# Output weights in half tiles from another queue, and loads and output products moved in program order, in the two feed-forwards of a two-layer block

## The chip, the cores and the metric

The kernel runs on one core of one Trainium2 chip. The metric is device time in microseconds, lower is better. Before the change three timed runs gave 1641.31, 1640.96 and 1637.72 us, median 1640.96.

## What is computed

A block of two layers works on 512 image positions `h` and 256 context positions `hc`, each of 1024 features, in float32. Each layer has a mixer (layer 0: a chunk MLP beside differential attention; layer 1: windowed attention with sinks) and a feed-forward. The change touches the feed-forwards alone:

```python
FFN_HIDDEN = ((8 * D_MODEL + 3 * 256 - 1) // (3 * 256)) * 256     # 2816
def swiglu(h, w_in, w_out):
    g, u = jnp.split(h @ w_in, 2, axis=-1)
    return (jax.nn.silu(g) * u) @ w_out
...
h = h + g2 * swiglu(modulate(h, norm2_g[l], sh2, sc2), ffn_w_in[l], ffn_w_out[l])
if need_ctx:                                                      # layer 0 only
    hc = hc + cg2 * swiglu(modulate(hc, norm2_g[l], csh2, csc2), ffn_w_in[l], ffn_w_out[l])
```

So layer 0's feed-forward has 768 columns (512 and 256), layer 1's 512.

## The kernel before

**Precision.** TensorE multiplies `float32r` tiles. Every float32 operand is split into a high part, which ScalarE makes by a copy that rounds, and a low part, the difference, which GpSimd or VectorE subtracts. One product of a 128-column block is then three matmuls (`mm3`, lines 100 to 102): high by high, high by low, low by high.

**Hidden features.** The 2816 hidden features are 22 groups of 128, numbered f. What the description of the change calls a pair is one f: the gate and the value columns of 128 hidden features, 1 MB of weights in one `raw` tile of 2048 columns, loaded on SyncE's queue by `ffn_in` (line 804). Layer 0 has two buffers for these tiles, layer 1 three (two in one pool, and one in the ring for each f with f % 3 == 2). Pairs 0 and 1 (layer 1: 0 to 2) go the direct way. All others use Strassen's scheme in Winograd's form: seven products, numbered 1 to 7, each of four column blocks, on half of the positions (384 columns in layer 0, 256 in layer 1). Their weights are `a11`, `a12`, `a21`, `a22` and four sums of them, which VectorE forms in `weights` (line 968). `slot` (lines 910 to 918) makes the high and low part of each: ScalarE's copy on line 913, the subtraction on line 917. There are 8 such slots in layer 0 and 12 in layer 1, so weights are made ahead of their products.

**Evacuations in a pair.** Products 1, 6, 7 and 4 accumulate in one half of a PSUM tile (`pw`), 5 and 3 in the other. Between them the running sum is read: after 1 on lines 996 and 997, after 5 on line 1005, after 6 on line 1001, after 3 on line 1008, after 7 on line 1012, after 4 on line 1017. The next product into the same half has to wait for that reading. After product 4 the hidden tile of the pair is split on lines 116 and 117 (`hh`).

**Output products.** `s2(g, m)` multiplies the two pairs 2g and 2g+1 with the block m (of 8) of the output weights, first the 512 positions, in layer 0 then the 256 of the context, and adds the result to the residual on line 766. Their weights come through `load` (lines 923 to 926): one `rawo` tile of 1024 columns (512 KB) for four m, in one buffer in layer 0 and two in layer 1, on SyncE's queue. `s2_weights` asks for it at m % 4 == 0 and makes a slot of 512 columns at every even m.

**Order.** For f from 3 to 21 a string gives the order in which products and output blocks are written down: `2156ab37cd4` for even f and `2a1b56c3d74` for odd f, where a digit is a product and a letter an output block (two at f = 3). The order on each engine is not this one, though: the program is built with `schedule_with_timeline_sim=True`, so a planner with a simulated clock of its own lays out each engine's queue, with the written order as its priority. What is ready in the plan can move ahead of what isn't. `tc.issue_after(ins)` binds this: an instruction in the block that runs on the same engine as `ins` is put behind `ins` in that engine's queue. At run time each queue is fixed.

**Beside it.** In layer 0's loop VectorE also computes the modulation of layer 1 (`ada_dot`, line 222) from 48 loads of 512 KB on SyncE's queue (line 216).

Of the kernel before, what the change touches and what calls it, by code (L numbers as in the profile page):

```python
# [6 lines left out]
F32 = mybir.dt.float32  # L7
F32R = mybir.dt.float32r
# [6 lines left out]
P = 128  # L15
# [6 lines left out]
NF = HID // P  # L22
# [4 lines left out]
class Builder:  # L27
# [821 lines left out]
    def ffn(self, l):  # L849
        tc, nc, a = self.tc, self.nc, self.a  # L850
        both = l == 0
# [4 lines left out]
        ring = tc.alloc_tile_pool(name=f"ring_f{l}", bufs=1, side="left", reuse_waits="tile")  # L856
        if both:

            for n, shape, bufs in (("rawo", [P, 1024], 1), ("hs", [P, T], 1), ("u", [P, NH], 1), ("w", [P, 1024], 5)):
                ring.tile(shape, F32, name=self.uid(n), tag=n, bufs=bufs)  # L860
        whos = ((0, TX), (TX, TC))[:2 if both else 1]
        todo = [(1, j, k) for j in range(6) for k in range(KT)] if both else []
# [47 lines left out]
        def slot(src, t=None):  # L910
            t = wtile() if t is None else t
            with tc.issue_after(self.first_sq.ins) if (3, 8)[l] <= self.nslot < 12 else ExitStack():
                nc.scalar.copy(t[:, 0, :], src)  # L913
# [3 lines left out]
            eng.tensor_tensor(t[:, 1, :], src, t[:, 0, :].bitcast(F32), ALU.subtract)  # L917
            return t
# [1 line left out]
        self.nslot = self.nw = 0  # L920
        self.first_sq = self.last_sq

        def load(src, cols):
            t = ring.tile([P, cols], F32, name=self.uid("rawo"), tag="rawo", bufs=(1, 2)[l])
            nc.sync.dma_start(t, src)
            return t

        def raw(f):
            return self.raws.pop(f) if f < 2 else self.ffn_in(l, f, ring if l and f % 3 == 2 else self.Rf)
# [26 lines left out]
            self.split(*hid[-1], gates.pop(f), nc.gpsimd)  # L956

        def weights(n, f):
            if f not in raws:
                raws[f] = raw(f)  # L960
                sums[f] = self.sumsq()[:, :512] if f % 3 == 2 else self.tmp("t")
            r, t = raws[f], sums[f]
            a11, a12, a21, a22 = [r[:, i * 512:(i + 1) * 512] for i in range(4)]
            for v, x, y, how in ((5, a21, a22, ALU.add), (6, t, a11, ALU.subtract), (3, a12, t, ALU.subtract),
                                 (7, a11, a21, ALU.subtract)):
                if v == n:
                    with tc.issue_after(self.last_diag.ins) if both and f < 3 and n == 5 else ExitStack():
                        nc.vector.tensor_tensor(t, x, y, how)  # L968
            return slot({1: a11, 2: a12, 4: a22}.get(n) if n in (1, 2, 4) else sums[f])
# [7 lines left out]
        def product(n, f):  # L977

            w = weights(n, f)
            st = state.setdefault(f, {})  # L980
            if n == 2:
                st["p2"] = (self.fill if f < 3 else self.bank)()[:, :NH]
                out = st["p2"]
            elif n == 1:
                w_ = self.wide()
                st["w"] = [w_[:, :NH], w_[:, 512:512 + NH]]
                out = st["w"][0]
            else:
                out = st["w"][n in (5, 3)]
            for j in range(4):  # L990
                c = slice(j * P, (j + 1) * P)
                self.mm3(out, (w[:, 0, c], w[:, 1, c]), op[n][j], j == 0 and n in (1, 2, 5), j == 3)
            ps0, ps1 = st.get("w", (None, None))
            if n == 1:
                g = st["g"] = self.gated_tile(ring if f % 3 == 2 else None)
                nc.scalar.copy(g[:, :NH], st["p2"])
                ins = nc.vector.tensor_tensor(g[:, :NH], g[:, :NH], ps0, ALU.add)
                more(1, f, ins)
                nc.scalar.activation(g[:, :NH], g[:, :NH], AF.Silu)
            elif n == 6:  # L1000
                nc.scalar.copy(st["g"][:, NH:], ps0)
            elif n == 5:
                own = f % 3 == 2
                st["u"] = ring.tile([P, NH], F32, name=self.uid("u"), tag="u", bufs=1) if own else self.tmp()[:, :NH]
                nc.scalar.copy(st["u"], ps1)
            elif n == 3:
                g = st["g"]
                ins = nc.vector.tensor_tensor(g[:, NH:], g[:, NH:], ps1, ALU.add)  # L1008
                more(3, f, ins)
                nc.scalar.activation(g[:, NH:], g[:, NH:], AF.Silu)  # L1010
            elif n == 7:
                ins = nc.vector.tensor_tensor(st["u"], st["u"], ps0, ALU.add)  # L1012
                more(7, f, ins)
                nc.vector.tensor_tensor(st["g"][:, NH:], st["g"][:, NH:], st["u"], ALU.mult)
            elif n == 4:
                g = st["g"]
                self.last_s1 = nc.vector.tensor_tensor(g[:, :NH], g[:, :NH], ps0, ALU.mult)
                hi, lo = self.hidden(F32R), self.hidden(F32R)
                if f < NF - 1:
                    self.split(hi, lo, g, nc.gpsimd)  # L1020
                else:
                    self.split(hi[:, NH:], lo[:, NH:], g[:, NH:])
                    self.split(hi[:, :NH], lo[:, :NH], g[:, :NH])
                hid.append((hi, lo))
                del state[f], raws[f], sums[f]
                more(4, f, self.last_s1)
# [5 lines left out]

        def s2_weights(g, m):

            if m % 4 == 0:
                outs[g] = load(a["ffn_out"][l, g, :, 256 * m:256 * m + 1024], 1024)
                if g == NF // 2 - 1:
                    f = NF + m // 4
                    pool = ring if l and f % 3 == 2 else self.Rf
                    self.big = pool.tile([P, 2048], F32R, name=self.uid("raw"), tag="raw", bufs=1 if pool is ring else 2)  # L1040
# [12 lines left out]

        hid, outs, w2, Wl = [], {}, {}, []

        nd = (2, 3)[l]
        self.direct_mm, self.gated = [], []
# [14 lines left out]
        for v in ("5 6 22 12 52 62 32 7 72 4 h 42", "5 6 d 4 7 h")[l].split():  # L1072
# [331 lines left out]
```

## Time and profile before

| | |
|---|---|
| timed runs, median | 1640.96 us (1637.72 to 1641.31) |
| profiled execution, span from first to last instruction | 1641.9 us (no time of its own is given beside the span) |
| mean granted clock of TensorE over the span | 0.977 |
| layer 0's loop | about 456 to 960 us of the span |
| layer 1's loop | about 1290 to 1600 us of the span |
| HBM read | 158.29 MB |

In the rows of the profile an instruction is named by its engine and its line in the kernel: PE is TensorE, PEld its weight loads, DVE VectorE, ACT ScalarE, POOL GpSimd, SP SyncE; `SPq` and `ACTq` are instructions that issue transfers. Names such as `w<-raw` say that a tile `w` is written from a tile `raw`. A bracket `[5.31 <-DMA raw<-ffn_in]` says how long the engine stood idle before the instruction and what ended that. In a view of waits, one row is "who <- whom: total us, times, longest us".

### The profile page before, as it was taken

What the parts mean: (1) busy time and instruction counts of PE and PEld (TensorE: products, weight loads), DVE (VectorE), ACT (ScalarE), POOL (GpSimd) and SP (SyncE); (2) the same over time, 40 slices, a digit from 0 to 9 for tenths busy, and PEclk for the clock granted to TensorE, in tenths of its full rate; (3) what the DMA queues carried; (4) which work ended last, traced back from release to release, by engine and by line L of the source; (5) the groups of instructions that cost most, each with busy time, mean ns of one, the idle gap of its engine ahead of it and who ended that gap; (6) DMA issues with size and microseconds to landing.
All of it is one profiled execution on the core that took longest, in us unless ns stands there. A gap on an engine that the chain in (4) does not pass through costs nothing.

```text
span 1641.9 us, 24642 instructions
## 1 busy us (share of the span) xinstructions
PE 1542.8 (94%) x9547; PEld 1367.1 (83%) x9547; DVE 1073.0 (65%) x1980; ACT 724.5 (44%) x1472; POOL 766.9 (47%) x543
## 2 busy tenths in 40 slices
PE   6999989999999999999999988999989999999996
PEld 4776877899899889998989978777868989898886
DVE  4621788756857788666665585665667857666665
ACT  2423675645533233333333244555664544444443
POOL 0463221062157666666666316532222466675662
PEclk9999989999999999999999999999999999999998
DMA  8744100141223343343432012110233222322201
GB/s 317 298 153 169 40 7 1 65 139 68 76 79 116 105 139 131 105 150 126 142 131 77 27 51 91 52 33 25 74 116 123 65 103 92 101 90 103 90 27 52
DMA packets 47957, 161.98 MB, mean 99 GB/s; under 512 B 5472, under 2 KB 9952, under 8 KB 40160
## 3 DMA queue, kind: packets, MB, share of 16 engines
q1 hardware_dynamic: 47696, 160.28, 28.4%
q8 instruction: 75, 1.23, 0.3%
q14 instruction: 42, 0.34, 0.1%
q10 hardware_dynamic: 144, 0.13, 0.0%
HBM read 158.29 MB, written 2.10 MB: 98 GB/s over the span
## 4 chain that ended last, share of the span: by engine, by line
PE 69%; DVE 11%; POOL 6%; DMA 5%; ACT 4%; issue 3%; POOLq 0%; SPq 0%; DVEq 0%; ACTq 0%
PE pw L100 9%; PE pw L101 9%; PE pw L102 9%; PE pb L100 7%; PE pb L101 7%; PE pb L102 7%; POOL w L917 5%; DMA raw<-ffn_in 3%; PE pf L100 3%; PE pf L101 2%; PE pf L102 2%; PE pb L1257 2%; PE pb L1246 2%; PE pf L351 2%; DVE t L968 2%
## 5 line engine op out<-in xcount | busy, mean ns | idle before, releaser
L100 PE MATMUL pw<-ax,w 128*128 128x384 f32 (+2 forms) x732 | 237.5, 328 | 16.1 <-DVE q L1012 6.7
L101 PE MATMUL pw<-ax,w 128*128 128x384 f32 (+2 forms) x732 | 237.9, 325 | 4.1 <-DVE ax L458 2.5
L78 POOL TENSOR_TENSOR w<-raw,w 128x512 fp32r<-128x512 f32 (+1 forms) x84 | 127.6, 1526 | 243.2 <-ACT w L75 220.8
L102 PE MATMUL pw<-ax,w 128*128 128x384 f32 (+2 forms) x732 | 236.7, 325 | 2.1 <-POOL w L917 2.1
L917 POOL TENSOR_TENSOR w<-raw,w 128x512 fp32r<-128x512 f32 x119 | 177.7, 1507 | 54.2 <-ACT w L913 53.4
L917 POOL TENSOR_TENSOR w<-t,w 128x512 fp32r<-128x512 f32 x90 | 133.4, 1482 | 139.9 <-ACT w L913 136.5
L100 PE MATMUL pb<-hh,w 128*128 128x512 f32 x480 | 167.3, 362 | 12.8 <-ACT hh L116 8.3
L766 DVE SCALAR_TENSOR_TENSOR xT<-pb,mod,xT 128x512 f32<-128x512 f32 (+3 forms) x208 | 144.5, 704 | 43.8 <-PE pb L102 43.1
L101 PE MATMUL pb<-hh,w 128*128 128x512 f32 x480 | 171.2, 358 | 0.5 <-POOL hh L117 0.5
L102 PE MATMUL pb<-hh,w 128*128 128x512 f32 x480 | 170.7, 357 | 0.0
L100 PEld LDWEIGHTS pw<-ax,w 128*128 128x128 f32 x732 | 142.0, 195 | 27.2 <-DVE q L1012 8.1
L100 PE MATMUL pw<-T,w 128*128 128x384 f32 (+1 forms) x508 | 159.1, 314 | 4.8 <-DVE hs L1008 2.4
L101 PE MATMUL pw<-T,w 128*128 128x384 f32 (+1 forms) x508 | 158.6, 312 | 4.0 <-DVE T L117 4.0
L102 PE MATMUL pw<-T,w 128*128 128x384 f32 (+1 forms) x508 | 158.2, 312 | 0.0
L101 PEld LDWEIGHTS pw<-ax,w 128*128 128x128 f32 x732 | 142.6, 195 | 12.1 <-DVE ax L458 3.4
L102 PEld LDWEIGHTS pw<-ax,w 128*128 128x128 f32 x732 | 142.4, 195 | 6.0 <-POOL w L917 2.7
L913 ACT CAST w<-t 128x512 fp32r<-128x512 f32 x104 | 64.5, 621 | 176.8 <-DVE t L968 122.5
L917 POOL TENSOR_TENSOR w<-rawo,w 128x512 fp32r<-128x512 f32 x63 | 94.1, 1493 | 66.5 <-ACT w L913 66.5
L100 PEld LDWEIGHTS pb<-hh,w 128*128 128x128 f32 x480 | 89.5, 189 | 27.0 <-ACT hh L116 10.8
L100 PEld LDWEIGHTS pw<-T,w 128*128 128x128 f32 x508 | 97.2, 192 | 9.7 <-DVE hs L1008 3.9
L101 PEld LDWEIGHTS pw<-T,w 128*128 128x128 f32 x508 | 97.4, 192 | 6.6 <-DVE T L117 4.6
L102 PEld LDWEIGHTS pb<-hh,w 128*128 128x128 f32 x480 | 90.3, 188 | 13.1
(363 smaller groups left out, 4056.7 us busy)
## 6 DMA issues: line engine op xcount, KB each, us to landing
raw<-ffn_in SPq DMA_DIRECT2D x44, 1024.0 KB, 4.9
ar<-ada SPq DMA_DIRECT2D x24, 1024.0 KB, 7.3
ar<-ada SPq DMA_DIRECT2D x48, 512.0 KB, 3.5
rawo<-ffn_out SPq DMA_DIRECT2D x44, 512.0 KB, 3.9
raw<-odd_out SPq DMA_DIRECT2D x32, 256.0 KB, 2.7
raw<-qk SPq DMA_DIRECT2D x16, 256.0 KB, 7.9
raw<-uv SPq DMA_DIRECT2D x16, 256.0 KB, 2.7
raw<-even_out SPq DMA_DIRECT2D x8, 512.0 KB, 4.2
```

Source lines behind the costliest of these rows:

```text
L78: eng.tensor_tensor(lo, raw, hi.bitcast(F32), ALU.subtract)
L100: mm(out, s[0], m[0], start=start, stop=False, **kw)
L101: mm(out, s[0], m[1], start=False, stop=False, **kw)
L102: return mm(out, s[1], m[0], start=False, stop=stop, **kw)
L351: nc.tensor.matmul(ps[32 * q:32 * q + 32, :w], cst[:, k, :], t[:, w * q:w * q + w], start=k == 0, stop=k == KT - 1, skip_group_check=True)
L766: self.nc.vector.scalar_tensor_tensor(h, ps[:, r], self.modcol(l, j, m, who), h, ALU.mult, ALU.add)
L913: nc.scalar.copy(t[:, 0, :], src)
L917: eng.tensor_tensor(t[:, 1, :], src, t[:, 0, :].bitcast(F32), ALU.subtract)
L968: nc.vector.tensor_tensor(t, x, y, how)
L1246: last = nc.tensor.transpose(pt[:, x * P:(x + 1) * P], es[2 * (x % 2) + x // 2][:, kb * P:(kb + 1) * P], self.ident)
L1257: nc.tensor.matmul(po[64 * h:64 * h + 64, :], V[vb][:, 64 * g:64 * g + 64], t[:, h * TC:h * TC + TC], start=kb == 0, stop=kb == nb - 1, sk ...
```

## The change

Three things, all in `ffn`. **Half tiles**: output weights are loaded in tiles of 512 columns (256 KB), two buffers in layer 0 and six in layer 1. One half is asked for ahead of the loop in layer 0, six in layer 1, and then one at each even m: in layer 0 before the slot of that m is made, from ScalarE's queue and behind the latest high-part copy of `slot` (`last_hi`); in layer 1 after it, from SyncE's queue. **Pairs ahead**: at the top of the loop body for f the weights of pair f+1 (layer 0) or f+2 (layer 1) are asked for; at f = 3 pairs 3 and 4, or 3 to 5. These loads are put behind the last weight load of the mixer (`last_w`) on SyncE's queue. **Program order**: every output product is put behind the last matmul of the product that is written ahead of it (`last_mm`) on TensorE. The outputs of the last two pairs (letters e to j, `s2_part` without `s2`) are not bound.

```diff
-            for n, shape, bufs in (("rawo", [P, 1024], 1), ("hs", [P, T], 1), ("u", [P, NH], 1), ("w", [P, 1024], 5)):
+            for n, shape, bufs in (("rawo", [P, 512], 2), ("hs", [P, T], 1), ("u", [P, NH], 1), ("w", [P, 1024], 5)):
...
-                nc.scalar.copy(t[:, 0, :], src)
+                self.last_hi = nc.scalar.copy(t[:, 0, :], src)
...
-        def load(src, cols):
-            t = ring.tile([P, cols], F32, name=self.uid("rawo"), tag="rawo", bufs=(1, 2)[l])
-            nc.sync.dma_start(t, src)
-            return t
+        def load():
+            g, c = halves.pop(0)
+            t = ring.tile([P, 512], F32, name=self.uid("rawo"), tag="rawo", bufs=nrawo)
+            with tc.issue_after(self.last_hi.ins) if both else ExitStack():
+                (nc.scalar if both else nc.sync).dma_start(t, a["ffn_out"][l, g, :, c:c + 512])
+            outs.append(t)
...
-            if f not in raws:
-                raws[f] = raw(f)
+            if f not in sums:
+                if f not in raws:
+                    raws[f] = raw(f)
                 sums[f] = self.sumsq()[:, :512] if f % 3 == 2 else self.tmp("t")
...
-                self.mm3(out, (w[:, 0, c], w[:, 1, c]), op[n][j], j == 0 and n in (1, 2, 5), j == 3)
+                self.last_mm = self.mm3(out, (w[:, 0, c], w[:, 1, c]), op[n][j], j == 0 and n in (1, 2, 5), j == 3)
...
-            if m % 4 == 0:
-                outs[g] = load(a["ffn_out"][l, g, :, 256 * m:256 * m + 1024], 1024)
-                if g == NF // 2 - 1:
+            if m % 4 == 0 and g == NF // 2 - 1:
...
-                w2[g] = slot(outs[g][:, m % 4 * 256:m % 4 * 256 + 512], t)
+                if both and halves:
+                    load()
+                w2[g] = slot(outs.pop(0), t)
+                if not both and halves:
+                    load()
...
-        def s2(g, m):
+        def s2(g, m, after):
 
             W = s2_weights(g, m)
-            for off, n in whos:
-                s2_part((2 * g, 2 * g + 1), m, W, off, n)
+            with tc.issue_after(after.ins):
+                for off, n in whos:
+                    s2_part((2 * g, 2 * g + 1), m, W, off, n)
...
+        nrawo = (2, 6)[l]
+        halves = [(g, c) for g in range(NF // 2) for c in range(0, 2048, 512)]
...
         for f in range(3, NF):
+            with tc.issue_after(self.last_w.ins):
+                for i in range(f if f == 3 else f + 1 + l, min(f + 2 + l, NF)):
+                    raws[i] = raw(i)
+                for _ in range(nrawo - both if f == 3 else 0):
+                    load()
...
-                        s2(*todo_m.pop(0))
+                        s2(*todo_m.pop(0), self.last_mm)
```

More of the change, by code (lines that the diff above doesn't have):

```diff
@@ L1033, in s2_weights @@
         def s2_weights(g, m):
-            if m % 4 == 0:
-                outs[g] = load(a["ffn_out"][l, g, :, 256 * m:256 * m + 1024], 1024)
-                if g == NF // 2 - 1:
-                    f = NF + m // 4
-                    pool = ring if l and f % 3 == 2 else self.Rf
-                    self.big = pool.tile([P, 2048], F32R, name=self.uid("raw"), tag="raw", bufs=1 if pool is ring else 2)
+            if m % 4 == 0 and g == NF // 2 - 1:
+                f = NF + m // 4
+                pool = ring if l and f % 3 == 2 else self.Rf
+                self.big = pool.tile([P, 2048], F32R, name=self.uid("raw"), tag="raw", bufs=1 if pool is ring else 2)
             if m % 2 == 0:
@@ L1043, in s2_weights @@
                 t = self.big[:, o:o + 1024].rearrange("p (a b) -> p a b", a=2) if g == NF // 2 - 1 else None
-                w2[g] = slot(outs[g][:, m % 4 * 256:m % 4 * 256 + 512], t)
+                if both and halves:
[3 more added lines that the diff above has]
+                    load()
             w = w2[g]
             return [(w[:, 0, c:c + P], w[:, 1, c:c + P]) for c in range(m % 2 * 256, m % 2 * 256 + 256, P)]
-        def s2(g, m):
+        def s2(g, m, after):
             W = s2_weights(g, m)
-            for off, n in whos:
-                s2_part((2 * g, 2 * g + 1), m, W, off, n)
-        hid, outs, w2, Wl = [], {}, {}, []
+            with tc.issue_after(after.ins):
+                for off, n in whos:
+                    s2_part((2 * g, 2 * g + 1), m, W, off, n)
+        hid, outs, w2, Wl = [], [], {}, []
+        nrawo = (2, 6)[l]
+        halves = [(g, c) for g in range(NF // 2) for c in range(0, 2048, 512)]
         nd = (2, 3)[l]
```

## The prediction

> **What bounds the kernel now.** I read the header of the page first, then the table by windows, and only then the waits.
>
> ```profile
> span 1641.9 us, 24642 instructions
> PE 1542.8 (94%) x9547; PEld 1367.1 (83%) x9547; DVE 1073.0 (65%) x1980; ACT 724.5 (44%) x1472; POOL 766.9 (47%) x543
> ```
>
> TensorE is busy 94% of the span, so what the change can bring is time in which TensorE stands still or runs slowly in the two feed-forwards. The table by windows sizes that. Its columns are the window, its length, and for PE, PEld, DVE, ACT and POOL the busy time with the count of instructions, then the granted clock, DMA share and GB/s. The first and third rows are stretches without a stall, the second and fourth are the parts of layer 0 and layer 1 that the edited loop fills, and the last lies behind one stall.
>
> ```profile
> 640.00:690.00 50.00, 50.00 (x288) 47.31 (x287) 34.70 (x52) 17.87 (x32) 32.61 (x22) 1.00 0.40 142
> 456.00:960.00 504.00, 487.76 (x2745) 456.94 (x2745) 345.30 (x516) 171.59 (x311) 304.38 (x197) 0.99 0.33 110
> 1361.00:1394.00 33.00, 33.00 (x230) 30.78 (x229) 22.75 (x34) 15.31 (x33) 22.30 (x17) 1.00 0.27 96
> 1290.00:1600.00 310.00, 296.37 (x1990) 272.80 (x1989) 201.00 (x287) 135.46 (x280) 203.40 (x145) 0.99 0.26 87
> 557.00:563.60 6.60, 5.86 (x18) 5.67 (x19) 1.44 (x4) 2.08 (x4) 3.13 (x2) 0.50 0.24 79
> ```
>
> Without a stall layer 0 takes 50.00/288 = 0.1736 us a matmul, so its 2745 would take 476.6 us of the 504: 27.4 us are lost, 16.2 of them idle (504 - 487.8). Layer 1 takes 33.00/230 = 0.1435 us, so 1990 take 285.5 of 310: 24.5 us are lost, 13.6 of them idle. The rest goes mostly in stretches like the last row, at a granted clock of 0.50. A microsecond of idle time thus stands for 27.4/16.2 = 1.7 us in layer 0 and 24.5/13.6 = 1.8 us in layer 1, and the **stock** that the change can draw on is 51.9 us.
>
> Who ended the idle time is in the waits of PE in these two windows (total, times, longest); three rows of layer 0, then four of layer 1:
>
> ```profile
> PE pb L100 <- ACT hh L116: 8.3, 6, 2.9
> PE pb L100 <- ACT hs L996: 4.1, 4, 1.6
> PE pw L100 <- ACT hs L1001: 1.8, 1, 1.8
> PE pw L100 <- DVE q L1012: 6.2, 3, 2.5
> PE pw L100 <- DVE u L1012: 4.7, 2, 2.4
> PE pw L100 <- DVE hs L1008: 1.8, 3, 0.8
> PE pw L100 <- ACT u L1005: 0.8, 1, 0.8
> ```
>
> No row names a weight or a DMA; they name short evacuations (L996 to L1017) and the split of the hidden tile (L116). The timeline shows why those are late, here for the wait at 1418 us:
>
> ```profile
> 1408.38 0.33 SPq L925 DMA_DIRECT2D rawo<-ffn_out  x1
> 1409.63 0.33 SPq L804 DMA_DIRECT2D raw<-ffn_in  x1
> 1416.99 0.69 DVE L968 TENSOR_TENSOR t<-raw 128x512 f32<-128x512 f32 x1 [5.31 <-DMA raw<-ffn_in]
> 1417.60 0.41 DVE L1012 TENSOR_TENSOR q<-q,pw 128x256 f32<-128x256 f32 x1
> 1418.07 0.39 PE L100 MATMUL pw<-ax,w 128*128 128x256 f32 x1 [2.53 <-DVE q L1012]
> ```
>
> DVE stood 5.31 us before L968, the sum of a later pair's weights, until its load landed. L1012, for which TensorE waited, is the next instruction on DVE and starts as soon as L968 is through. So the bound is **an urgent evacuation queued behind an operation that waits for a transfer**.
>
> **The change part by part.** *Layer 1, half loads.* The chain of waits gives the first and the last of four such loads in layer 1 (the one above is the second), and one of layer 0; the DMA issues (count, size, median to landing) give the usual times:
>
> ```profile
> 1342.64 7.43 DMA raw<-ffn_in
> ...
> 1542.53 7.04 DMA raw<-ffn_in
> ...
> 747.07 6.89 DMA raw<-ffn_in
> raw<-ffn_in SPq DMA_DIRECT2D x44, 1024.0 KB, 4.9
> rawo<-ffn_out SPq DMA_DIRECT2D x44, 512.0 KB, 3.9
> raw<-odd_out SPq DMA_DIRECT2D x32, 256.0 KB, 2.7
> ```
>
> The four took 7.0 to 7.4 us in place of 4.9, and a 512 KB `rawo` load had left 1.25 us ahead of the one above. Half the size ahead of it should leave half of the 2.4 us: 1.2 us. Four of the five waits on L1012 (10.9 us in all) become shorter by 4 x 1.2 = 4.8 us idle, 8.6 with the slow clock at 1.8. Bounds: nothing, if the same stalls turn up at other places, and all of it, 10.9 x 1.8 = 19.6. I take **-7**, between 4.8 and 8.6, since not every such wait need be followed by a slow stretch.
>
> *Layer 0, ScalarE.* Three waits follow a cast of `rawo` that stands in ACT's queue until its load lands:
>
> ```profile
> 606.59 0.62 ACT L913 CAST w<-rawo 128x512 fp32r<-128x512 f32 x1 [2.17 <-DMA rawo<-ffn_out]
> 609.34 0.85 PE L100 MATMUL pb<-hh,w 128*128 128x512 f32 x3 [1.28 <-ACT hh L116]
> 705.37 0.62 ACT L913 CAST w<-rawo 128x512 fp32r<-128x512 f32 x1 [1.96 <-DMA rawo<-ffn_out]
> 706.42 0.44 PE L100 MATMUL pw<-ax,w 128*128 128x384 f32 x1 [1.82 <-ACT hs L1001]
> 898.97 0.62 ACT L913 CAST w<-rawo 128x512 fp32r<-128x512 f32 x1 [1.14 <-DMA rawo<-ffn_out]
> 900.38 0.85 PE L100 MATMUL pb<-hh,w 128*128 128x512 f32 x3 [1.12 <-ACT hh L116]
> ```
>
> With one buffer of 1024 columns the next load cannot start before the last subtraction on the old one. With two halves the next is asked for one cast earlier: the loop's 19 pairs take 504 us and two halves each, so 13 us ahead, against 2.7 us for 256 KB. These waits should go: 1.28 + 1.82 + 1.12 = 4.2 us idle, 7.1 with the slow clock. Bounds 0 and 7.1; I take **-6**, since another wait may then be the last to end.
>
> *Layer 0, DVE.* The same picture as in layer 1 stands behind two waits on L116:
>
> ```profile
> 557.74 1.44 PE L100 MATMUL pb<-hh,w 128*128 128x512 f32 x3 [2.86 <-ACT hh L116]
> 753.99 0.69 DVE L968 TENSOR_TENSOR t<-raw 128x512 f32<-128x512 f32 x1 [2.77 <-DMA raw<-ffn_in]
> 756.06 0.85 PE L100 MATMUL pb<-hh,w 128*128 128x512 f32 x3 [2.35 <-ACT hh L116]
> ```
>
> The load took 6.89 us, 2.0 more than 4.9; half of it back, twice, is 2.0 idle, 3.4 at 1.7. Bounds 0 and 5.2 x 1.7 = 8.8. I take **-3**.
>
> *End of layer 1.* The chain waits there for the last output weights:
>
> ```profile
> 1576.93 3.67 DMA rawo<-ffn_out
> ```
>
> Six halves instead of two whole tiles let them start earlier. What TensorE lost there is the 0.8 on L1005 and the longest wait on L1008, 0.8: **-1.6** (bounds 0 and 1.6).
>
> *Weights asked for ahead.* In the waits of SyncE's queue in layer 0 (total, times, longest) the pair loads (L804) already wait for the buffer, not for being asked:
>
> ```profile
> SPq L804 <- POOL w L917: 24.4, 13, 3.3
> ```
>
> 13 pair loads of the loop's 19 leave at the moment when GpSimd frees the tile. The buffer count is unchanged, so asking one or two pairs ahead can start few of them sooner: **0**. What covers the loads is that weights are prepared well ahead (no row of PE's waits names one); without that each pair would wait up to 4.9 us.
>
> *ScalarE's issues.* Layer 0 issues 44 half loads from ACT. The one DMA that ACT issues now is this:
>
> ```profile
> 50.74 0.39 ACTq L303 DMA_DIRECT2D q<-lqk  x1
> L917 POOL TENSOR_TENSOR w<-t,w 128x512 fp32r<-128x512 f32 x52 | 80.9, 1556 | 81.1 <-ACT w L913 81.0
> ```
>
> 44 x 0.39 = 17 us more on an engine that is busy 171.6 us of 504. Queued behind each are the casts, evacuations and hidden splits of ACT. PE lost 14.2 us (8.3 + 4.1 + 1.8) to 171.6 us of ACT, 8%, so 17 us cost 1.4. The issue also waits until GpSimd has read the half two back; the second row (POOL idle 81 us for ACT's casts) says GpSimd runs close behind ACT, and the issue is put behind the latest cast, so that wait is mostly over. At worst each issue stands for one GpSimd operation, 44 x 1.56 = 69 us, 8% of it 5.5. I take **+2**, range 0 to 7.
>
> *Output products in program order.* The fence on PE adds no semaphore wait; it forbids that output matmuls run ahead of the pair's own products. Gain: at most the 8.3 us on L116, already mostly counted. Loss: products 1, 6, 7 and 4 share one accumulator, and between them TensorE needs other work while ACT and DVE read it. The nearest row for an uncovered read is L1008, 1.8/3 = 0.6 us; for all 38 pairs of the two loops that would be 22.8 us. Output matmuls now also stand between 6 and 3 and between 7 and 4, where they cover. I take one pair in six: **+4**, range -8 to +23.
>
> Sum: -7 - 6 - 3 - 1.6 + 0 + 2 + 4 = **-11.6 us** on the profiled span of 1641.9, 1630.3. The median of the timed runs is 0.9 below that span, so 1640.96 - 11.6 = **1629** us.
>
> One rule speaks against a part of this sum. The Trainium skill, "DMA: Bandwidth & Descriptors", section "Issuing engines are not separate DMA queues", says that transfers started from ScalarE and SyncE run on the same DMA engines and interleave, so that a second issuer saves only issue time. The rows above are all of one issuer and cannot show it for layer 0. By it the -3 of layer 0 would be nothing, and the sum -8.6.
>
> **The rivals.**
>
> *No change.* Halves are two loads of 2.7 in place of one of 3.9, so the pair load may meet just as much traffic, and L968 stands before L1012 because the plan of the build put it there, which the edit does not forbid. Then -7 and -3 fall away: -6 - 1.6 + 2 + 4 = -1.6, **1639**. This is also the case in which asking ahead does nothing. For it: the waits of layer 1 recur in one pattern, every 66 us, so they come from the plan. Against it: the landing must be late for a wait, and the one shown was late behind a whole `rawo`. The same page, section "Measured (HBM→SBUF, 128 partitions, SWDGE, issued from GpSimd)", advises transfers of 1 MiB and more, which speaks for this rival; no run here shows it for halves yet.
>
> *Most stalls go.* L968 no longer lands in front of an evacuation: -19.6 - 7.1 - 8.8 - 1.6 + 2 = -35, **1606**. For it: the stall-free rows above, at a clock of 1.00. Against it: DVE and ACT keep every operation that waits.
>
> *Slower: the outputs no longer fill in.* Before, output matmuls may run wherever a product's accumulator is being read; fenced, TensorE has nothing else when the next product isn't ready. It decides when the cover of 12 product matmuls (12 x 0.1435, 1.7 us in layer 1) is shorter than the way through ACT and DVE, where L1012 alone takes 0.41, and their queues. Price: 38 x 0.6 = 22.8, with +2 for ScalarE, less 6, 3 and 1.6, and layer 1's -7 not had: +14.2, **1655**. For it: layer 1's L1012 waits already follow a row of products without outputs. Against it: in the stall-free stretches PE is busy 33.00 of 33.00 us with the same products.
>
> **How the numbers follow.** Forecast 43%, most stalls go 13%, no change 22%, slower 22%. The forecast's own range is 1620 to 1636. About 0.2% (3.3 us) is what a measurement of this kernel can tell from no change: faster is 0.43 + 0.13 + 0.06 of the middle case, which spreads over the line at 1637.7, **0.62**; within, **0.13**; slower, 0.22 + 0.03, **0.25**. Half of each end case lies outside 1608 to 1655, 0.07 + 0.11, so that is the range.
>
> **What would show it.** Right: PE's waits on L1012 in layer 1 fall from 10.9 to about 6 us; no wait on L1001 or L116 behind a `rawo` cast; layer 0's window loses about 7 us, layer 1's about 5 to 9; pair loads still leave when GpSimd frees them, usually in 4.9 us. Wrong: pair loads still land in 7 us in front of an evacuation; ACT stands at its own DMA issues waiting for POOL; PE idles in many small pieces on L997, L1001, L1008 or L1012; or DVE's waits on `raw` turn up at other instructions with the same total.

## The result, and the profile after

After the change the kernel takes **1653.85 us** (median of 4 runs, 1652.18 to 1656.48), before it 1639.47 (4 runs, 1637.72 to 1641.31): ratio 1.0083, 95% interval 1.0064 to 1.0102. It is 14.4 us slower where the prediction said 12 us faster. The time lies inside the range, 1 us from the rival "the outputs no longer fill in" (1655).

The header of the page after, then its table by windows for the same two stretches (columns as in the prediction):

```profile
span 1654.7 us, 24721 instructions
PE 1543.4 (93%) x9547; PEld 1359.4 (82%) x9547; DVE 1080.7 (65%) x1980; ACT 724.2 (44%) x1472; POOL 775.4 (47%) x543
```

```profile
456.00:960.00 504.00, 479.05 (x2656) 444.65 (x2656) 338.49 (x495) 163.81 (x298) 314.54 (x196) 0.99 0.33 108
1290.00:1600.00 310.00, 291.40 (x1960) 264.62 (x1959) 206.01 (x288) 138.56 (x283) 199.48 (x142) 1.00 0.26 86
```

TensorE does the same work (1543.4 us busy against 1542.8), but in the same 504 us of layer 0 it gets through 2656 matmuls instead of 2745, in layer 1's 310 us through 1960 instead of 1990. At the prediction's 0.1736 and 0.1435 us a matmul these would be 15.5 and 4.3 us, but the windows are fixed in time, and the later kernel has other work in them. The last matmul of product 7 is cleaner: it ends at 937.8 us before and 947.4 after in layer 0, at 1612.2 and 1625.1 in layer 1, so most of the loss lies in layer 0.

Where it stands is in the groups by line. Four groups hold the first matmuls (line 100) of the edited loops, and some from other parts of the program: `pw<-T` are products 5, 6 and 7, `pw<-ax` 1, 3 and 4, `pb<-ax` product 2, `pb<-hh` the outputs. A row gives busy time, mean ns, then the idle time ahead of the group and what ended it. Before:

```profile
L100 PE MATMUL pw<-ax,w 128*128 128x384 f32 (+2 forms) x732 | 237.5, 328 | 16.1 <-DVE q L1012 6.7 <-DVE u L1012 4.7 <-ACT hs L1001 1.8
L100 PE MATMUL pb<-hh,w 128*128 128x512 f32 x480 | 167.3, 362 | 12.8 <-ACT hh L116 8.3 <-ACT hs L996 4.1 <-DVE xT L766 0.2
L100 PE MATMUL pw<-T,w 128*128 128x384 f32 (+1 forms) x508 | 159.1, 314 | 4.8 <-DVE hs L1008 2.4 <-ACT T L116 1.6 <-ACT u L1005 0.8
L100 PE MATMUL pb<-ax,w 128*128 128x256 f32 (+1 forms) x320 | 98.0, 307 | 0.9 <-DVE ctxT L766 0.8
```

After (the lines have moved by three: L999 and L1000 evacuate after 1, L1008 after 5, L1004 after 6, L1011 after 3, L1015 after 7, L1020 after 4):

```profile
L100 PE MATMUL pw<-ax,w 128*128 128x384 f32 (+2 forms) x732 | 234.1, 324 | 8.5 <-DVE q L1015 3.7 <-ACT ax L194 1.6 <-ACT hs L1004 1.5
L100 PE MATMUL pb<-hh,w 128*128 128x512 f32 x480 | 167.1, 358 | 1.3 <-DVE xT L766 1.2
L100 PE MATMUL pw<-T,w 128*128 128x384 f32 (+1 forms) x508 | 164.0, 323 | 36.0 <-ACT q L1008 13.1 <-DVE hs L1011 9.7 <-DVE hs L1000 8.8
L100 PE MATMUL pb<-ax,w 128*128 128x256 f32 (+1 forms) x320 | 98.3, 308 | 5.4 <-ACT w L913 2.9 <-DVE ctxT L766 2.4
```

The waits that the prediction wanted shorter are shorter: those on L116 (8.3) are gone, those on L1012 (6.7 + 4.7, now L1015) are 3.7 + 1.2. Which part of the change did that is settled below. The loss is in one group, **products 5, 6 and 7: 4.8 us idle became 36.0**. In layer 0's window PE's waits (total, times, longest) are led by

```profile
PE pw L100 <- ACT q L1008: 9.3, 8, 2.7
PE pw L100 <- DVE hs L1000: 7.3, 7, 2.4
...
PE pw L100 <- ACT u L1008: 2.3, 3, 1.1
```

The timeline shows one of them; start and length in us, and in brackets the idle time before:

```profile
661.20 0.34 PE L102 MATMUL pw<-T,w 128*128 128x384 f32 x1
661.37 0.83 ACT L116 CAST hh<-hs 128x768 fp32r<-128x768 f32 x1 [1.20 <-DVE hs L1020]
662.11 0.47 ACT L1008 COPY q<-pw 128x384 f32<-128x384 f32 x1
662.63 0.44 PE L100 MATMUL pw<-T,w 128*128 128x384 f32 x1 [1.10 <-ACT q L1008]
```

The first row is the last matmul of product 5, the last row the first of product 6. Nothing stands between them on TensorE, so it waits 1.10 us while ScalarE finishes L116 and then copies what 5 left. The copy reads the half that 5 wrote, and 6 writes **the other half**. The description of the kernel ahead of the prediction had said that only the next product into the same half waits; in the program as it is built the wait goes by the whole tile, so six of a pair's seven products (1, 5, 6, 3, 7, 4) form one chain with an evacuation between every two.

In layer 1 the longest total is on L1011, the sum after 3 (8.6 us in eight waits). Each time that sum is the next instruction on VectorE behind a weight sum (L971) that stood 0.7 to 2.4 us for GpSimd's subtraction (L917). It is the prediction's picture of an urgent evacuation in a queue behind something that waits, here for GpSimd in place of a transfer.

**Theory.** Each product on the tile waits for the evacuation of the one before it. Free outputs, and products of the neighbouring pair, stood between them before; the fence with the letters `2156ab37cd4` and `2a1b56c3d74` leaves nothing between 5 and 6. Counted from the order of the built programs, with 2.0 us wanted between two products in layer 0 and 1.4 in layer 1 (a choice, a little under one product's 12 matmuls, 2.1 and 1.7), the matmul time that is missing, summed over 39 pairs, is (layer 0 and layer 1):

```text
              between 5 and 6    all five steps
before          1.4    0.0         15.9    3.6
after          30.7   13.8         41.8   20.8
```

**Rivals.** The change's other parts (ScalarE's issues, half loads, early requests) cost the time; or an order by hand costs by itself, whatever stands between the products.

### The profile page after: what moved, and what is told of

It reads as the page before. It is cut to its first block, busy times and chain, and to the rows that moved or that the text cites. A ratio compares the mean times of both kernels' runs of the same rounds, so it can differ in the third digit from the quotient of the medians.

```text
span 1654.7 us, 24721 instructions
## 1 busy us (share of the span) xinstructions
PE 1543.4 (93%) x9547; PEld 1359.4 (82%) x9547; DVE 1080.7 (65%) x1980; ACT 724.2 (44%) x1472; POOL 775.4 (47%) x543
## 4 chain that ended last, share of the span: by engine, by line
PE 63%; DVE 16%; POOL 6%; ACT 6%; issue 5%; DMA 4%; ACTq 0%; POOLq 0%; SPq 0%; DVEq 0%
PE pw L100 8%; PE pw L101 7%; PE pw L102 7%; PE pb L100 7%; PE pb L101 7%; PE pb L102 7%; POOL w L917 4%; DMA raw<-ffn_in 3%; PE pf L100 2%; PE pf L101 2%; PE pf L102 2%; PE pb L1270 2%; PE pb L1259 2%; DVE t L971 2%; DVE junk L222 2%
## 5 line engine op out<-in xcount | busy, mean ns | idle before, releaser
L100 PE MATMUL pw<-ax,w 128*128 128x384 f32 (+2 forms) x732 | 234.1, 324 | 8.5 <-DVE q L1015 3.7
L101 PE MATMUL pw<-ax,w 128*128 128x384 f32 (+2 forms) x732 | 234.6, 321 | 2.7 <-DVE ax L458 1.4
L102 PE MATMUL pw<-ax,w 128*128 128x384 f32 (+2 forms) x732 | 233.1, 320 | 0.0
L917 POOL TENSOR_TENSOR w<-t,w 128x512 fp32r<-128x512 f32 x90 | 129.3, 1437 | 159.6 <-ACT w L913 142.5
L917 POOL TENSOR_TENSOR w<-raw,w 128x512 fp32r<-128x512 f32 x119 | 177.6, 1505 | 49.7 <-ACT w L913 46.7
L100 PE MATMUL pw<-T,w 128*128 128x384 f32 (+1 forms) x508 | 164.0, 323 | 36.0 <-ACT q L1008 13.1
L766 DVE SCALAR_TENSOR_TENSOR xT<-pb,mod,xT 128x512 f32<-128x512 f32 (+3 forms) x208 | 144.0, 703 | 44.5 <-PE pb L102 44.2
L101 PE MATMUL pw<-T,w 128*128 128x384 f32 (+1 forms) x508 | 159.1, 313 | 2.9 <-DVE T L117 2.9
L102 PE MATMUL pw<-T,w 128*128 128x384 f32 (+1 forms) x508 | 158.9, 313 | 0.0
L100 PEld LDWEIGHTS pw<-ax,w 128*128 128x128 f32 x732 | 138.7, 190 | 21.7 <-DVE q L1015 5.4
L101 PEld LDWEIGHTS pw<-ax,w 128*128 128x128 f32 x732 | 139.3, 190 | 11.0 <-DVE ax L458 3.1
L102 PEld LDWEIGHTS pw<-ax,w 128*128 128x128 f32 x732 | 139.3, 191 | 3.0
L100 PEld LDWEIGHTS pw<-T,w 128*128 128x128 f32 x508 | 97.7, 192 | 50.0 <-ACT q L1008 17.2
L117 POOL TENSOR_TENSOR hh<-hs,hh 128x768 fp32r<-128x768 f32 (+1 forms) x42 | 80.5, 1917 | 70.6 <-ACT hh L116 69.2
L100 PE MATMUL pb<-ax,w 128*128 128x256 f32 (+1 forms) x320 | 98.3, 308 | 5.4 <-ACT w L913 2.9
L917 POOL TENSOR_TENSOR w<-rawo,w 128x512 fp32r<-128x512 f32 x63 | 94.1, 1494 | 18.4 <-ACT w L913 18.4
L102 PEld LDWEIGHTS pb<-hh,w 128*128 128x128 f32 x480 | 90.3, 188 | 13.9
```

The source lines that it names most:

```text
L100: mm(out, s[0], m[0], start=start, stop=False, **kw)
L101: mm(out, s[0], m[1], start=False, stop=False, **kw)
L102: return mm(out, s[1], m[0], start=False, stop=stop, **kw)
L117: return (lo_eng or nc.vector).tensor_tensor(lo, src, hi.bitcast(F32), ALU.subtract)
L766: self.nc.vector.scalar_tensor_tensor(h, ps[:, r], self.modcol(l, j, m, who), h, ALU.mult, ALU.add)
```

## The experiments

All ran with the kernel before on the same chip. e1 to e4, e5 to e8 and e9 to e12 each shared one chip, so a difference in us between these sets, or with the kernel after, goes across chips. "idle" is the sum of the four groups above, from one profiled execution each; e10's took 1607.66 us and e8's 1624.15, off their medians.

| kernel | us, median | ratio to before (95%) | idle, us |
|---|---|---|---|
| before | 1639.5 to 1642.3 | 1 | 34.6 |
| after | 1653.85 | 1.0083 (1.0064 to 1.0102) | 51.2 |
| e1 after, no fence | 1635.33 | 0.9965 (0.9953 to 0.9977) | 36.1 |
| e2 before, with fence | 1658.67 | 1.0106 (1.0087 to 1.0125) | 46.4 |
| e3 after, one output a gap | 1671.16 | 1.0181 (1.0166 to 1.0196) | 60.3 |
| e4 before, pairs ahead | 1639.13 | 0.9988 (0.9975 to 1.0000) | 36.2 |
| e5 after, two tiles | 1612.75 | 0.9821 (0.9796 to 0.9846) | 18.5 |
| e6 after, fence one earlier | 1641.41 | 1.0001 (0.9982 to 1.0020) | 41.9 |
| e7 after, every step covered | 1628.02 | 0.9911 (0.9890 to 0.9932) | 31.5 |
| e8 e1, SyncE's queue | 1630.23 | 0.9923 (0.9899 to 0.9946) | 26.6 |
| e9 before, two tiles | 1615.19 | 0.9852 (0.9830 to 0.9875) | 21.8 |
| e10 e5, no fence | 1599.71 | 0.9761 (0.9738 to 0.9784) | 14.1 |
| e11 e10, SyncE's queue | 1603.51 | 0.9776 (0.9757 to 0.9796) | 14.2 |
| e12 e5, SyncE's queue | 1614.60 | 0.9838 (0.9816 to 0.9859) | 23.6 |

### The parts of the change: e1, e2, e4

e1 is the kernel after, with the outputs free again:

```diff
-            with tc.issue_after(after.ins):
+            with ExitStack():
                 for off, n in whos:
```

> The whole change but for the fence: output matmuls may again run ahead of the pair's own products. Theory (the fence takes the cover from the products of one pair, which wait for each other's evacuation): the loss goes, 1632 to 1641 us, and PE's waits on the copies and sums of products 1, 5 and 3 are back to a few us in the two loops (31 us in the changed kernel on these three, 4.1 + 2.4 + 0.8 on them before). Rival A (the half loads from ScalarE's queue, or the reshuffled loads, cost the time): still 1650 to 1658. Rival B (asking ahead): still 1650 to 1658.

e2 is the kernel before with that fence alone (`last_mm` and `issue_after` in `s2`, nothing else).

> The kernel before with the fence alone: whole output tiles on SyncE's queue, pairs asked for as before. Theory: 1652 to 1665 us, as slow as the changed kernel or slower, with the same waits on the evacuations of 5, 3 and 1. Rivals A and B: within 3 us of the kernel before, 1637 to 1643.

e4 is the kernel before with the early requests alone (the loop at the top of the body for f, without the half loads).

> The kernel before with the pairs' weights asked for 1 or 2 pairs ahead, nothing else. The order on SyncE's queue changes by two loads at the start of layer 1. Theory: no change, 1636 to 1643 us, since pair loads leave when their buffer is freed. Rival B: 1648 us or more.

The fence costs 18.5 us beside the rest of the change (1653.85 - 1635.33, across chips) and 17.8 without it (1658.67 - 1640.86, the kernel before on that chip). The rest of the change gains 5.5 us (1640.86 - 1635.33), asking ahead nothing that can be told. The group of products 5, 6 and 7 follows the fence; e1, then e2 (where L1005 is the copy after 5):

```profile
L100 PE MATMUL pb<-hh,w 128*128 128x512 f32 x480 | 167.4, 361 | 19.4 <-ACT hh L116 13.0 <-ACT hs L999 4.0 <-DVE xT L766 2.1
L100 PE MATMUL pw<-T,w 128*128 128x384 f32 (+1 forms) x508 | 159.1, 313 | 6.3 <-DVE hs L1011 4.0 <-DVE hs L1000 1.8 <-ACT T L116 0.5
```

```profile
L100 PE MATMUL pb<-hh,w 128*128 128x512 f32 x480 | 166.9, 357 | 1.3 <-DVE xT L766 1.2
L100 PE MATMUL pw<-T,w 128*128 128x384 f32 (+1 forms) x508 | 163.1, 321 | 34.6 <-ACT q L1005 12.1 <-DVE hs L997 8.5 <-DVE hs L1008 8.1
```

They also show who removed the waits on L116: not the half loads (13.0 us in e1, more than before) but the fence, which keeps an output from running up against a hidden tile that isn't split yet. It saves them and pays more elsewhere. The waits on the sum after 7, 11.4 us before, are 4.2 with the fence alone (e2) and 6.8 with the rest alone (e1), so either shortens them.

### Same fence, other places for the outputs: e3, e6, e7

e3 puts one output after each product from 5 on:

```diff
-            for v in ("2156ab37cd4", "2a1b56c3d74", ...
+            for v in ("215a6b3c7d4", "215a6b3c7d4", ...
```

> The whole change with the fence kept, and the written order of pairs 3 to 20 changed to 215a6b3c7d4 for even and odd f, so that an output block stands between each product and the next that uses the same accumulator tile from 5 on. By the program's order the matmul time that is missing between two products of one tile falls from 41.8 to 9.4 us in layer 0 and from 20.8 to 3.7 us in layer 1 (counted against 2.0 and 1.4 us a step). Theory: the waits on 5 to 6 and 7 to 4 go, 1625 to 1638 us. Rivals A and B, or a fence that costs through anything but cover: 1648 to 1658.

A miss: it is the slowest kernel of all. The count behind that expectation had left out that the evacuation after 1 (a copy of product 2, then the sum with 1) needs product 2 as well, and here 2, 1 and 5 follow one another in every pair. The wait went there:

```profile
L100 PE MATMUL pw<-T,w 128*128 128x384 f32 (+1 forms) x508 | 165.8, 327 | 55.2 <-DVE hs L1000 46.3 <-ACT u L1008 3.8 <-DVE hs L1011 3.6
```

The wait for 5's evacuation (13.1 + 4.3 us in the kernel after) is down to 3.8 + 1.0, as it should be with an output between 5 and 6. In layer 1 some 12 us of the waits on L1000 also stand behind a weight sum (L971) that waited for its load. So the time speaks against the theory unless that hole in the count explains it; e7 closes the hole: there the next pair's products 2 and 1 (N and M) are written at the end of this pair.

```diff
-            for v in ("2156ab37cd4", "2a1b56c3d74", "2a1b56c3de7f4ghij", "2a1b56c3de7f4g")[...]:
+            for v in ("21" if f == 3 else "") + ("5a6b3c7NdM4", "5a6b3c7N4Md", "5a6b3cde7f4ghij", "5a6b3cde7f4g")[...]:
...
+                elif v in "NM":
+                    product(2 if v == "N" else 1, f + 1)
```

> The kernel after with its fence, but the order by hand rewritten: products 2 and 1 of the next pair are asked for at the end of this pair, and one output stands between every two products on the tile. Missing matmul time by the same count, now with product 2 counted as well: 5 us and 2 us. Theory (only cover counts): 1620 to 1638, likeliest 1630; PE's waits on L1000, L1008, L1011 and L1015 under 10 us in all. Open is the hidden tile, which the first output of every second pair needs one product earlier than before: waits on L116 of up to 2 us in ten pairs a layer would bring it to 1645. Rival (order by hand costs by itself): 1648 or more, with the four rows at over 25 us.

Within the expectation, 26 us less than after with the same fence. The waits on the four lines sum to 16.7 us, more than the 10 hoped for, and product 2 now waits 7.8 us for outputs that VectorE has not read yet (L766):

```profile
L100 PE MATMUL pb<-hh,w 128*128 128x512 f32 x480 | 169.3, 359 | 1.9 <-DVE xT L766 1.4 <-ACT hh L116 0.2
L100 PE MATMUL pw<-T,w 128*128 128x384 f32 (+1 forms) x508 | 158.7, 313 | 15.4 <-DVE hs L1000 5.0 <-DVE hs L1011 5.0 <-ACT u L1008 4.6
```

e6 loosens the fence of the kernel after by one product:

```diff
-                        s2(*todo_m.pop(0), self.last_mm)
+                        s2(*todo_m.pop(0), self.prev_mm)   # last matmul of the product before the last one
```

> The kernel after, with the fence one product looser: output matmuls may not run ahead of the last product but one, where they may not run ahead of the last product in the kernel after. So the planner can again put outputs between two products on one tile. Counted from the program's order as before (matmul time missing between one product and the next on its tile, 2.0 us wanted in layer 0, 1.4 in layer 1): 22 us and 3 us, against 42 and 21 in the kernel after and 18 and 4 without the fence. Theory: 1633 to 1643, likeliest 1637. Rival (any fence on outputs costs, since they are no longer free to fill a random gap): between the two, 1643 to 1652.

Within the expectation: 12 us of the fence's 18 come back. Against before it stands at 1.0001, e1 at 0.9965, and the intervals don't touch: a rest of some 6 us remains. In its rows the waits on 5's evacuation (L1009 here) are 0.5 us, those on 1's (L1001) 11.0, and those on L116 are back:

```profile
L100 PE MATMUL pb<-hh,w 128*128 128x512 f32 x480 | 167.2, 359 | 16.4 <-ACT hh L116 12.6 <-ACT hs L1000 2.6 <-DVE xT L766 1.2
L100 PE MATMUL pw<-T,w 128*128 128x384 f32 (+1 forms) x508 | 159.3, 314 | 12.6 <-DVE hs L1001 11.0 <-DVE hs L1012 0.9 <-ACT u L1009 0.5
```

### One tile or two: e5, e9, e10

The plainest test leaves order and fence alone and takes away the sharing:

```diff
-                w_ = self.wide()
-                st["w"] = [w_[:, :NH], w_[:, 512:512 + NH]]
+                st["w"] = [self.wide()[:, :NH] for _ in range(2)]
```

> The kernel after, with one edit: each pair takes two PSUM tiles in place of the two halves of one, the first for products 1, 6, 7 and 4, the second for 5 and 3. Fence, letters, half loads and queues stay. Theory (a product waits for the evacuation of whatever was last written to its tile, the other half included, and the fence took away what stood between 5 and 6): the wait of 6 on the copy of 5 is no longer there, so PE's waits on L1008 (17.4 us) and the L1000 ones before 5 (8.8) nearly go; what stays uncovered is 4 behind 7 in odd pairs. 1626 to 1640, likeliest 1633. Rival A (the fence costs because outputs are late for something else, whatever the tiles): 1648 or more, the idle time reappearing at other rows. Rival B (two tiles a pair leave none free for the next pair, whose product 1 must wait for L1020 of this one): waits on L1020 of over 10 us and 1645 or more.

41 us less than after (across chips), below the range of the theory, and with the fence still in it 30 us faster than before. Products 5, 6 and 7, and the outputs:

```profile
L100 PE MATMUL pb<-hh,w 128*128 128x512 f32 x480 | 167.4, 358 | 1.4 <-DVE xT L766 1.3
L100 PE MATMUL pw<-T,w 128*128 128x384 f32 (+1 forms) x508 | 159.3, 314 | 13.4 <-DVE hs L1019 8.2 <-DVE hs L999 4.9 <-ACT hs L1003 0.2
```

The wait on 5's evacuation (L1007 here) has left this row. What remains, 8.2 us on L1019 (after 4), is a product that takes over a tile from the pair before: rival B's mechanism (though by the group the product is 5, 6 or 7, not 1), a little under its 10 us and without its price. Then the same edit in the kernel before:

> The kernel before with one edit: two PSUM tiles a pair in place of the halves of one. Nothing of the change is in it. Theory (a shared tile makes each product wait for the evacuation of the one before it; before, free outputs covered most of that, 3.5 us of L1005 and L1008 in the waits, and the rest of the loss was L116 and L1012 behind transfers, which stays): 1618 to 1632, likeliest 1625. Rival (the gain of the fifth run, 41 us against the kernel after, needs the rest of the change): 1634 or more.

26 us, beyond the expected range, because waits that were to stay went too, or moved:

```profile
L100 PE MATMUL pw<-ax,w 128*128 128x384 f32 (+2 forms) x732 | 232.9, 322 | 2.7 <-ACT ax L194 1.6 <-ACT ax L457 0.4 <-DVE u L1011 0.3
L100 PE MATMUL pb<-hh,w 128*128 128x512 f32 x480 | 166.3, 360 | 1.2 <-DVE xT L766 1.0
L100 PE MATMUL pw<-T,w 128*128 128x384 f32 (+1 forms) x508 | 159.2, 314 | 14.7 <-DVE hs L1016 11.1 <-ACT T L116 1.6 <-DVE hs L996 1.2
```

No output waits on L116, and of the waits on the sum after 7 (L1011 in this kernel) 0.6 us are left of 11.4. But the third group, 4.8 us before, has 14.7, 11.1 of them on L1016, the sum after 4: the tile taken over from the pair before, as in e5. And VectorE still stands for the pairs' loads in layer 1; its waits there, of before and then of e9:

```profile
DVE t L968 <- DMA raw<-ffn_in: 19.9, 4, 5.3
DVE sq L968 <- DMA raw<-ffn_in: 7.1, 2, 5.3
```

```profile
DVE t L968 <- DMA raw<-ffn_in: 16.3, 4, 5.0
DVE sq L968 <- DMA raw<-ffn_in: 5.4, 2, 4.8
```

27.0 us became 21.7, and TensorE still sees them, at the new place. All four waits on L1016 in layer 1 (7.3 us, where those on L1012 were 10.9 before) look like this one:

```profile
1330.91 0.69 DVE L968 TENSOR_TENSOR t<-raw 128x512 f32<-128x512 f32 x1 [4.99 <-DMA raw<-ffn_in]
1331.52 0.41 DVE L1016 TENSOR_TENSOR hs<-hs,pw 128x256 f32<-128x256 f32 x1
1331.99 0.38 PE L100 MATMUL pw<-T,w 128*128 128x256 f32 x1 [2.41 <-DVE hs L1016]
```

So the cost of the late transfers shrank by a third; it did not go with the shared tile. What went are the waits between two products of one pair, and in layer 0 those of the outputs. Two tiles also gave the planner another order: in layer 0 product 6 follows straight on 5 in 16 of 20 pairs, without a wait, and in the kernel before in none. How much of the 26 us is the wait itself and how much the new order, these runs do not separate.

> The fifth run's kernel (two tiles a pair, 1612.8 us) without the fence on outputs. Theory (with nothing to cover between 5 and 6 the fence has no price left, and it may even help, since outputs no longer run into L116): 1609 to 1618, no difference beyond the interval, with waits on L116 back at some 10 us. Rival (the fence costs its 18 us with any tiles): 1600 or less.

13 us less than e5, with intervals of the ratio that don't touch. The time meets the rival's 1600, if by 0.3 us, and the theory fails: with two tiles the fence still costs 13.0 us (across chips), or 11.1 on one chip (e12 less e11, below), against 17.8 and 18.5 with one. L116 does not come back:

```profile
L100 PE MATMUL pb<-hh,w 128*128 128x512 f32 x480 | 166.5, 360 | 1.6 <-DVE xT L766 1.4
L100 PE MATMUL pw<-T,w 128*128 128x384 f32 (+1 forms) x508 | 159.2, 314 | 10.2 <-DVE hs L1019 8.3 <-DVE hs L999 1.2 <-ACT hs L1003 0.7
```

These rows are of an execution that took only 3.8 us less than e5's, so they can't name the whole 13. Those of e11 and e12, without and with the fence (1601.48 and 1615.89 us), say more:

```profile
L100 PE MATMUL pw<-T,w 128*128 128x384 f32 (+1 forms) x508 | 158.5, 312 | 7.7 <-DVE hs L1019 5.3 <-DVE hs L999 1.2 <-ACT T L116 1.0
L100 PE MATMUL pw<-T,w 128*128 128x384 f32 (+1 forms) x508 | 160.3, 316 | 15.0 <-DVE hs L1019 10.0 <-DVE hs L999 5.0
```

Of the four groups' 9.4 us (23.6 - 14.2), 4.7 are waits on L1019 and 3.8 on L999. Two tiles take away the wait between 5 and 6, but not those after 1 and at the take-over, and outputs held back by the fence don't cover these either. So the mechanism, an evacuation without cover, stands, and the shared tile is only a part of it: some 12 of the fence's 18 us come without it.

e10 is the fastest kernel of the study: 0.9761 of before, with half loads, early requests and two tiles, and no order for the outputs. On the same chip it takes 15.5 us less than e9 (1615.19 - 1599.71). So the half loads and early requests, worth 5.5 us with the shared tile, are worth 15.5 with two.

### ScalarE's queue: e8, e11, e12

In e8, e11 and e12 the half loads of layer 0 are issued from SyncE's queue (for e1, e10 and e5):

```diff
-            with tc.issue_after(self.last_hi.ins) if both else ExitStack():
-                (nc.scalar if both else nc.sync).dma_start(t, ...)
+            with ExitStack():
+                nc.sync.dma_start(t, ...)
```

> The kernel of the first run (after without the fence, 1635.3 us) with layer 0's half loads issued from SyncE's queue in place of ScalarE's. Theory (the -6 of the waits behind rawo casts came from the halves, the queue alone gives the issue time of 44 x 0.39 us back to ScalarE at some 2 us): 1633 to 1636, no difference beyond the interval. Rival A (a half load behind the pair loads' waits in SyncE's queue starts late, so the queue is what brought the gain): 1638 to 1645, ScalarE's casts waiting for rawo again. Rival B (ScalarE's issues cost more than thought): 1630 or less.

> The tenth run's kernel with layer 0's half loads on SyncE's queue in place of ScalarE's. Theory now (ScalarE, which issues 44 half loads, stands at some of them for GpSimd's last read of the half, some 13 us in the first run, and some of that reaches TensorE): 3 to 7 us less than the tenth run. Rival (the eighth run's 5 us less was chance between two chips): within 2 us of it.

> The fifth run's kernel (fence, two tiles a pair) with layer 0's half loads on SyncE's queue. Theory: 1605 to 1611, as the eleventh run to 3 us, since neither the fence nor the queue meets an uncovered evacuation. Rival (fence and queue interact: fenced outputs need their weights at a fixed time, and a half load queued behind pair loads is late): 1613 or more, with ScalarE's casts waiting for rawo.

e8's ratio is below e1's, with intervals that don't touch: some 0.4%, 5 to 7 us, nearest to rival B. ScalarE does wait for GpSimd's read of the old half in e1, in five rows of layer 0's window, here the first and the last of them:

```profile
ACT hs L1004 <- POOL w L917: 2.7, 1, 2.7
...
ACT w L913 <- POOL w L917: 2.4, 1, 2.4
```

They sum to 12.9 us; in e8 one row of that kind is left, 5.0. Two of the waits reach TensorE, the first like this:

```profile
657.60 1.14 ACT L913 CAST w<-rawo 128x512 fp32r<-128x512 f32 x2 [2.69 <-DMA rawo<-ffn_out]
659.65 0.34 ACTq L927 DMA_DIRECT2D rawo<-ffn_out  x1
660.03 0.83 ACT L116 CAST hh<-hs 128x768 fp32r<-128x768 f32 x1 [1.28 <-POOL w L917]
660.91 1.03 PE L100 MATMUL pb<-hh,w 128*128 128x512 f32 x3 [2.36 <-ACT hh L116]
```

ScalarE stood 2.69 us for a half to land, then 1.28 for GpSimd at the issue of the next one, and the split L116 came behind both. At these two places (661 and 855 us) e1's outputs wait 2.36 and 2.38 us, e8's 0.96 each. That much idle time goes with the queue; whether the rest of e8's gain is the queue or the plan that came with it stays open.

With two tiles no difference between the queues can be told: e11 takes 3.8 us more than e10, e12's ratio is 0.0017 above e5's, and both pairs of intervals overlap. So e11's theory falls, and e12 misses its range by 3.6 us. Its time is in the rival's range (1613 or more), but without the late half loads that the rival named: ScalarE's waits for `rawo` in layer 0's window are 5.7 us.

## Why the prediction was wrong, point by point

- **Output products in program order, +4: the step that failed.** It measures +17.8 and +18.5 us, inside the term's own -8 to +23. "One pair in six", some six waits of 0.6 us, was a choice without a row behind it. In the trace after, products 5, 6 and 7 have 40 waits on the evacuations after 5, 3 and 1, 35.9 us in all; before they had 5, 3.2 us. The order by hand stood in the letters: 5 and 6 adjacent in every even and odd string, and nothing between them in 19 of 39 pairs of the built program after; and the outputs that the step saw between 7 and 4 stand there in even strings alone. The step also thought of 1, 6, 7 and 4 alone as sharing an accumulator, where 5 and 3 sit in the same tile and the same chain. That sharing is the smaller part of the price: with two tiles the fence still costs 11 to 13 us. The rival, at 22%, named the mechanism: short waits on evacuations without cover. Of the lines that the prediction gave for it, L997 and L1008 (now L1000 and L1011) came true; the largest, L1005 (now L1008), was not among them. That its 1655 is so near is partly luck: its 22.8 us for the fence was 4 to 5 too much, and the 8.6 it took off for the rest some 3 too much.
- **Gain "at most the 8.3 us on L116".** Right as a mechanism: the fence removes these waits (1.3 us idle ahead of the outputs in e2).
- **Layer 1, half loads, -7.** The waits on the sum after 7 fall from 11.4 us before to 4.6 + 2.2 = 6.8 in e1, close to the 4.8 us less that the step worked out. But the half loads, layer 0's and the end's terms and ScalarE's issues together were to bring -15.6, and e1 shows -5.5. With two tiles (e10 less e9) the same edits bring 15.5; the prediction was for the shared tile, so that is no hit.
- **Layer 0, ScalarE, -6, and DVE, -3.** Not had. ScalarE's waits for `rawo` at casts into `w` did fall, from 14.0 us in layer 0's window to 5.4 in e1, but those of the outputs on L116 rose from 8.3 to 13.0. In three of e1's five (8.3 us) ScalarE stands idle until VectorE's sum after 4; the other two (4.7 us) are those behind a late half and an issue. In e7, which places products and outputs otherwise, and in e9, whose planner does, they all but go, without smaller loads in e9.
- **ScalarE's issues, +2.** Within its 0 to 7: e8 against e1 puts it at 5 to 7, e11 against e10 at nothing.
- **Weights asked for ahead, 0.** Right: e4 is at 0.9988.
- **The bound.** "An urgent evacuation queued behind an operation that waits for a transfer" named the releasers rightly, and stopped one question early: why must TensorE wait for that evacuation at all? e9 answers a part: half of the 51.9 us of stock (26.1) goes with the shared tile, and not one load is moved. The bound itself is still there, 7.3 us in layer 1 of e9.
- **The factor 1.7 from idle time to lost time** doesn't hold from kernel to kernel: after lost 14.4 us for 16.6 more idle, e9 won 26.1 for 12.8 less.

Two places of the Trainium skill bear on this. "Perfetto Trace Analysis", section "Matmuls", asks that independent groups of matmuls rotate through PSUM banks, so that an evacuation lies beside the next group's matmuls. The runs agree in effect (26.1 us in e9), with one addition: two halves of one tile don't rotate in this program, since the wait goes by the tile. "DMA: Bandwidth & Descriptors", section "Issuing engines are not separate DMA queues", says that a second issuer saves only issue time. The rows agree, the same 256 KB landing in 3.1 us from both queues, and neither e8 nor e11 shows a gain from ScalarE's that is clear of the interval:

```profile
rawo<-ffn_out ACTq DMA_DIRECT2D x44, 256.0 KB, 3.1
rawo<-ffn_out SPq DMA_DIRECT2D x44, 256.0 KB, 3.1
```

## What to carry to other kernels

Before work is pinned to an order, write down for each accumulator what stands on TensorE between its last matmul and the next on the same tile, and compare that with the way through the evacuation: where a string of letters leaves nothing, that wait comes in every round. A wait has two ends: besides making the releaser earlier, ask whether the waiter needs it, since a second tile (one line here) brought 26 us, and the edits to loads and queues 5.5 without it and 15.5 on top of it. Then look where the waits went: here the tile taken over from the pair before cost 11.1 us of waits, 7.3 of them behind the same loads.

## What the runs showed of the hardware that had not been expected

Half a transfer does not land in half the time: 256 KB of `rawo` took 3.1 us, where the prediction had used 2.7, and 512 KB had taken 3.9. And a transfer that VectorE waits for can be late at little cost: the fence alone raised VectorE's waits for layer 0's pair loads from 20.6 + 3.5 us to the 40.8 + 20.1 us of these rows of e2,

```profile
DVE t L968 <- DMA raw<-ffn_in: 40.8, 11, 7.4
DVE sq L968 <- DMA raw<-ffn_in: 20.1, 5, 7.3
```

but followed back on VectorE, only one wait of TensorE on it in layer 0 lies behind such a load (0.71 us, at 576 us). That no row of TensorE's waits names L968 would not show this, since a row names the last releaser alone. In layer 1 of the same kernel three waits on L1012 (0.81, 1.11 and 0.83 us) do come directly behind an L968 that stood some 2 us for its load.
